# A two-layer decoder trunk: the opening norm taken channel by channel on transposed x, and the first residual read back from a stored copy

## The chip, the core and the metric

The kernel runs on one core of a Trainium2 chip. The metric is the device time of one execution in microseconds (us), and a kernel's time is the median of its runs. Engines are named as the profile names them: TensorE (PE; its weight loads are PEld), VectorE (DVE), ScalarE (ACT), GpSimd (POOL) and SyncE (SP), which only issues transfers.

## The reference, cut to what matters

`x` is 1024 positions by 1024 channels in float32. The trunk has two layers: a mixer and a gated MLP each, every one with an RMS norm ahead of it and a residual add behind it. The change concerns the first norm, the first projection and the first residual.

```python
def rmsnorm(x, g):
    xf = x.astype(jnp.float32)
    y = xf * lax.rsqrt(jnp.mean(xf * xf, axis=-1, keepdims=True) + EPS)
    return (y * g.astype(jnp.float32)).astype(x.dtype)

def even_mixer(x, ...):                    # x is rmsnorm of the stream here
    p = x @ w_in                           # 1024 -> 2560
    xa, ga, c_pre, b_post, vb = jnp.split(p, ...)          # 512 channels each
    xa = causal_depthwise_conv(xa, lru_conv_w, lru_conv_b)
    ya = rg_lru(xa, ...) * jax.nn.gelu(ga)
    yb = b_post * causal_depthwise_conv(c_pre * vb, sconv_w, sconv_b)
    return jnp.concatenate([ya, yb], axis=-1) @ w_out

x = x + even_mixer(rmsnorm(x, mix0_norm), ...)
x = x + conv_glu_ffn(rmsnorm(x, ffn_norm[0]), ...)
# then the same with odd_mixer (gated chunks and attention), and a last norm
```

The norm's factor belongs to a position, its gain `g` to a channel.

## The kernel before, in words

**Layout.** Activations are kept channels by positions: 8 groups of 128 channels on the partitions, 1024 positions along the free axis, worked on in two halves of 512 (`HALF[0]`, `HALF[1]`). TensorE multiplies in a reduced format (`fp32r`), so every operand is split in two, a high part (a rounding copy on ScalarE) and a low part (the remainder, a subtraction on VectorE), and a product is three matmuls: high by high, high by low, low by high. The normed stream's parts are `AH` and `AL`, both 128x8x1024. A projection of 128 output channels over one half is `proj_half` (L376): 8 channel groups times 3 matmuls of 512 columns, 24 in all. Small accumulators come from four banks (`psml`), large ones from two pairs of banks (`pbig`). `t2` gives 4 buffers of 512 columns, `t4` gives 4 of 1024.

**Weights.** `W` walks a list of weights in the order of their use. Raw weights (`wst`, 512 KB, two buffers) are asked of SyncE's queue (L106), which takes its transfers in order; ScalarE makes `wh`, VectorE `wl` (L129), three pairs of buffers. `W.get(key, depth)` prepares that many weights ahead.

**What sets the order.** The text is run by a scheduler that orders each engine's queue by its own costs and by the tiles' dependencies; the order within an engine is then fixed. `tc.issue_after` pins an instruction behind another. In the start, the order is written by hand: the string `START` lists steps (`q` squares, `r` root, `s` scale, `h` high, `l` low, `w` a weight ahead) with a block of 128 positions, and `WARM` puts matmuls of the identity (`warm`, L470) behind some of them, beside 14 at the very beginning.

**The start (`class Start`).** `x` arrives as 8 blocks of 128 positions by 1024 channels. For each block: ScalarE squares it into `xn` with the row sum in `sss` (L433), the reciprocal root follows in five small steps (L438 to L442), and VectorE scales the block by the factor of each position and the broadcast row `g0` of gains (L446). TensorE transposes the normed block in eight 128x128 pieces into two banks `xp` (L455), ScalarE writes the high parts `AH` from there (L459), VectorE the low parts `AL` (L464). `mix0` multiplies the first two projections (`0xa` and `0ga`) in quarters of 256 positions for the first half, then blocks 4 to 7 are normed while the first half of a third projection, `0cp0a`, is multiplied; then the second half of `0xa` and `0ga`, and `0cp0b`.

**Behind the start.** For each of four channel blocks the mixer makes a convolution over positions (`xc`, L402 and three taps at L405), its parts `xh` and `xl`, two block-diagonal gates from them (`ra`, `ix`, L1347, by weights `gwa` and `gwx`), a GELU of `0ga` (`gg`, L1369), and the projections `0cp`, `0vb` and `0bp`. The gate weights are put together in `t2` buffers: GpSimd clears them and issues four small loads (L1332), then the split makes `gwha`, `gwhx` and the low parts.

**The first output projection (`out_proj0`).** Its input is `Y`, split again into `AH` and `AL` (L370); 8 blocks of 128 output channels for each half. `Out.residual(oc)` loads 128 channels of `x` for all positions into `xc` (L546), TensorE transposes them in eight pieces (`xr`, L550), and ScalarE copies them to the stream's tile `hT_o` (L551). The eviction adds the product to the residual in place and stores it to `hdr` in DRAM (L557, L558), a tile of channels by positions. The second layer's `Out(1)` loads its residual from `hdr` already.

Of the kernel before, what the change touches and what calls it, by code (L numbers as in the profile page):

```python
# [16 lines left out]
P = 128  # L17
# [4 lines left out]
NH = 8  # L22
HD = 64
# [32 lines left out]
START = "q0 r0 s0 q1 r1 s1 h0 q2 l0 r2 s2 h1 l1 w1 q3 r3 s3 h2 l2 w2 h3 l3".split()  # L56

WARM = {"h0": 3, "h1": 3}
# [25 lines left out]
class Weights:  # L84
# [12 lines left out]
    def _dma(self, n=None):  # L97
        n = n or NWST + (self.more is not None)
        while self.n_dma < min(self.n_conv + n, len(self.plan) if self.limit is None else self.limit):
            key, ap = self.plan[self.n_dma]  # L100
            k, m = ap.shape[1], ap.shape[2]
            if self.more is not None and self.n_dma % 3 == 2:
                w = self.more.tile([P, DC, P], F32, tag="wst2", name=f"wst{self.n_dma}")
            else:
                w = self.pool.tile([P, DC, P], F32, tag="wst", bufs=NWST, name=f"wst{self.n_dma}")
            self.nc.sync.dma_start(w[:, :k, :m], ap)  # L106
            self.raw.append((w, k, m))
            self.n_dma += 1
# [11 lines left out]
    def ahead(self, depth=3):  # L120
# [14 lines left out]
        return did  # L135

# [20 lines left out]
def trunk(ctx: ExitStack, tc: tile.TileContext, x, mix0_norm, mix0_w_in, lru_conv_w, lru_conv_b,  # L157
# [111 lines left out]
    def load_rows(name, groups):  # L269
# [8 lines left out]
        t = cp.tile([P, n], F32, name=f"par_{name}")  # L278
        return t, offs, raw, n

    def turn_rows(t, offs, raw, n):
        ps = psml("pt")
        pe.transpose(ps[:, :n], raw[:n, :], ident[:n, :n])
        dve.tensor_copy(t, ps[:, :n])
# [131 lines left out]
    g0 = spl.tile([P, D], F32, name="g0")  # L416
    xs_, last = [], {}

    class Start:


        def __init__(self):
            self.ss = spl.tile([P, DC, 4], F32, name="sss")
            self.ys, self.ps = {}, {}

        def load(self, tt):
            xt = spl.tile([P, D], F32, tag="x", bufs=5, name=f"x{tt}")
            nc.sync.dma_start(xt, x[tt * P:(tt + 1) * P, :])
            xs_.append(xt)

        def squares(self, tt):
            y = self.ys[tt] = t4(f"xn{tt}")
            return act.activation(y, xs_[tt], AF.Square, accum_out=self.ss[:, tt, 0:1]), None  # L433

        def root(self, tt):
            sm = self.ss[:, tt]
            v, r, q = sm[:, 1:2], sm[:, 2:3], sm[:, 3:4]
            dve.tensor_scalar(v, sm[:, 0:1], 1.0 / D, EPS, op0=ALU.mult, op1=ALU.add)  # L438
            a = act.activation(r, v, AF.Abs_reciprocal_sqrt)
            dve.tensor_tensor(q, v, r, op=ALU.mult)  # L440
            dve.scalar_tensor_tensor(q, q, -0.5, r, op0=ALU.mult, op1=ALU.mult)
            return a, dve.scalar_tensor_tensor(r, q, 1.5, r, op0=ALU.add, op1=ALU.mult)  # L442

        def scale(self, tt):
            y = self.ys[tt]
            return None, dve.scalar_tensor_tensor(y, xs_[tt], self.ss[:, tt, 2:3], g0,  # L446
                                                  op0=ALU.mult, op1=ALU.mult)

        def high(self, tt):
            y, self.ps[tt] = self.ys.pop(tt), []  # L450
            for q_ in range(2):
                ps = psml(f"xp{tt}{q_}")
                for i in range(4):
                    c = 4 * q_ + i
                    pe.transpose(ps[:, i * P:(i + 1) * P], y[:, c * P:(c + 1) * P], ident)  # L455
                src = ps.rearrange("p (i t) -> p i t", i=4)
                at = slice(0, P), slice(4 * q_, 4 * q_ + 4), slice(tt * P, (tt + 1) * P)
                self.ps[tt].append((src, at))
                last["act"] = act.copy(AH[at], src)  # L459
            return last["act"], None  # L460

        def low(self, tt):
            for src, at in self.ps.pop(tt):
                last["dve"] = dve.tensor_tensor(AL[at], src, AH[at].bitcast(F32), op=ALU.subtract)  # L464
            return None, last["dve"]

        def warm(self, n):
            ps = psml("warm")
            for _ in range(n):
                pe.matmul(ps[:, :P], ident, ident, start=True, stop=True)  # L470

        def first(self):

            self.warm(14)
            steps = {"q": self.squares, "r": self.root, "s": self.scale, "h": self.high,
                     "l": self.low, "w": W.ahead}
            before = [None, None]
            for step in START:
                with ExitStack() as after:
                    for ins in before:  # L480
                        if ins is not None:
                            after.enter_context(tc.issue_after(ins.ins))
                    did = steps[step[0]](int(step[1:] or 0))
                before = [new or old for new, old in zip(did, before)]
                if step in WARM:
                    self.warm(WARM[step])

        def second(self, beside):


            steps = {"q": self.squares, "r": self.root, "s": self.scale, "h": self.high,
                     "l": self.low}

            def do(ops, *behind):
                for op in ops.split():
                    with ExitStack() as after:
                        for ins in behind:
                            after.enter_context(tc.issue_after(ins.ins))
                        steps[op[0]](int(op[1]))

            behind = last["act"], last["dve"]
            do("q4 r4 q5 r5 s4 h4 l4 q6 r6 s5 h5 l5 q7 r7 s6 s7", *behind)
            do("h6 l6 h7 l7", beside(*behind))
            turn_rows(*par_rows)
            sp_cm.__exit__(None, None, None)

    norm = [Start()]
    for tt in range(4):
        if tt == 3:
            W._dma(1)  # L510
        norm[0].load(tt)
        if tt == 0:
            nc.sync.dma_start(g0, mix0_norm.partition_broadcast(P))
    W._dma()
    par_rows = load_rows("a", [
        (r1(mix0_norm), 8), (lru_conv_w[0].rearrange("k (c p) -> (k c) p", p=P), 16),
# [5 lines left out]
    (o_n0, o_lw, o_lb, o_ba, o_bx, o_lam, o_sw, o_sb, o_n1, o_fn, o_fin, o_gb) = o  # L522
    gcols = {"mix0": cols(par, o_n0), "mix1": cols(par, o_n1), "ffn0": cols(par, o_fn),
             "ffn1": cols(par, o_fn + 8), "fin": cols(par, o_fin)}
    for tt in range(4, 8):
        norm[0].load(tt)
    norm[0].first()


    class Out:  # L530


        def __init__(self, ly):
# [3 lines left out]
            if ly:  # L537
# [5 lines left out]

        def residual(self, oc):
            xc = t4(f"xc{oc}").rearrange("p (n c) -> p n c", n=DC)
            nc.sync.dma_start(xc, x[:, oc * P:(oc + 1) * P].rearrange("(n p) c -> p n c", p=P))  # L546
            for h in range(2):
                ps = psml(f"xr{oc}{h}")
                for i in range(4):
                    pe.transpose(ps[:, i * P:(i + 1) * P], xc[:, 4 * h + i], ident)  # L550
                act.copy(self.hT[:, oc, HALF[h]], ps)  # L551
# [16 lines left out]
    def out_proj0(y_rest):  # L568
# [3 lines left out]
        o_.residual(0)  # L572
        for oc in range(DC):
            w = W.get(f"0o0{oc}")
            if oc < DC - 1:
                o_.residual(oc + 1)
# [698 lines left out]
    def mix0(norms):  # L1275


        ws = [W.get(k, 1) for k in ("0xa0", "0ga0")]
        pxa, pga = pbig("0xa0"), pbig("0ga0")
        for s in (slice(0, H // 2), slice(H // 2, H)):  # L1280
            for p_, w in zip((pxa, pga), ws):
                proj_half(p_[:, s], w, s)
        pc = [psml("0cp0a")]

        def beside(a, d):
# [604 lines left out]
```

## Time and profile before

| | |
|---|---|
| median of 3 runs | 2132.75 us (2132.11, 2132.75, 2134.26) |
| the profiled execution | 2131.98 us, of which the trace's span is 2130.3 |
| granted TensorE clock, mean | 0.999 |
| TensorE busy | 2093.4 us, 98% of the span, 9673 instructions |
| VectorE busy | 1599.0 us, 75% |
| ScalarE busy | 1068.4 us, 50% |
| GpSimd busy | 75.4 us, 4% |
| moved by the transfers | 249.98 MB, a mean of 117 GB/s |

Of the span, 60 us are the start and the first channel block's first projections, 190 more the rest of the first mixer, and from 255 to some 350 runs the first output projection; the other five sixths are the two MLPs, the second mixer and the last norm, which the change's steps don't touch. A row of an instruction reads: start in us, duration, engine, line, operation, output<-inputs, shape, and in brackets how long the engine had waited and what ended the wait. A row of a group has a count, the minimum, median and maximum duration in ns, and the time from the first to the last. A row of a stretch has its bounds, its length, then busy time (and instructions) of PE, PEld, DVE, ACT and POOL, the granted clock, the share of the 16 DMA engines and the GB/s.

### The profile page before, as it was taken

The page shows a single profiled execution, that of the slowest core. Times are in us where ns is not written, and L with a number is a line of the kernel's source. Part 1 is how long each engine was busy: PE and PEld are TensorE (multiplying, and loading weights), DVE is VectorE, ACT ScalarE, POOL GpSimd, SP SyncE. Part 2 cuts the span into 40 slices and gives each one's busy share as a digit, 9 for nine tenths or more (in the row PEclk, how much of TensorE's full clock was granted, in tenths as well). Part 3 has the DMA queues.
Part 4 walks back from the last instruction along what each step waited for, and adds up shares of the span by engine and source line. Part 5 has one row for each costly group of instructions (what it writes and reads, how often), then busy time and mean ns, then how long its engine had stood idle before and what let it go on. Part 6 is the DMA issues. An engine that isn't in the chain of part 4 may idle for free. (4 is left out here: it accounts for less than half of the span.)

```text
span 2130.3 us, 25849 instructions
## 1 busy us (share of the span) xinstructions
PE 2093.4 (98%) x9673; PEld 1719.2 (81%) x9673; DVE 1599.0 (75%) x2290; ACT 1068.4 (50%) x1493; POOL 75.4 (4%) x121
## 2 busy tenths in 40 slices
PE   8999999999999999999999999999999999999998
PEld 7888888788888888888778888788788888878887
DVE  6655647998888777875566766868998888777875
ACT  5333534654555555333556575744655455555323
POOL 0000001000000000000111111101000000000000
PEclk9999999999999999999999999999999999999999
DMA  4111342333323267752221212442333233267732
GB/s 150 56 50 41 108 154 94 95 113 109 104 96 107 80 206 253 242 173 74 75 58 54 75 56 59 156 153 89 104 104 119 94 116 97 80 228 248 240 104 80
DMA packets 269318, 249.98 MB, mean 117 GB/s; under 512 B 10224, under 2 KB 222000, under 8 KB 269192
## 3 DMA queue, kind: packets, MB, share of 16 engines
q1 hardware_dynamic: 268856, 247.83, 36.5%
q8 instruction: 76, 1.25, 0.2%
q0 software_dynamic: 192, 0.30, 0.1%
q14 instruction: 50, 0.41, 0.1%
q10 hardware_dynamic: 144, 0.20, 0.0%
HBM read 181.93 MB, written 64.26 MB: 116 GB/s over the span
## 5 line engine op out<-in xcount | busy, mean ns | idle before, releaser
L129 ACT CAST wh<-wst 128x1024 fp32r<-128x1024 f32 (+1 forms) x87 | 86.3, 992 | 223.4 <-PE op L376 45.2
L129 DVE TENSOR_TENSOR wl<-wst,wh 128x1024 fp32r<-128x1024 f32 (+1 forms) x87 | 100.0, 1150 | 96.6 <-ACT wh L129 96.5
L676 PE MATMUL X<-TH,wh 128*128 128x512 f32 x384 | 150.0, 391 | 1.8 <-ACT u L1034 1.4
L676 PE MATMUL X<-TH,wl 128*128 128x512 f32 x384 | 149.7, 390 | 0.7 <-DVE wl L370 0.7
L676 PE MATMUL X<-TL,wh 128*128 128x512 f32 x384 | 149.4, 389 | 0.0
L369 ACT CAST wh<-wst 128x1024 fp32r<-128x1024 f32 x96 | 100.3, 1051 | 74.6 <-PE YZ L676 49.5
L370 DVE TENSOR_TENSOR wl<-wst,wh 128x1024 fp32r<-128x1024 f32 x96 | 116.5, 1218 | 11.9 <-ACT wh L369 11.9
L698 DVE SCALAR_TENSOR_TENSOR cg<-g,par_c,cg 128x1023 f32<-128x1023 f32 x88 | 112.8, 1281 | 7.3 <-ACT cg L692 6.1
L698 DVE SCALAR_TENSOR_TENSOR cv<-v,par_c,cv 128x1023 f32<-128x1023 f32 (+1 forms) x88 | 112.4, 1277 | 0.0
L676 PE MATMUL YZ<-AH,wh 128*128 128x512 f32 x240 | 93.5, 389 | 0.0
L676 PE MATMUL YZ<-AL,wh 128*128 128x512 f32 x240 | 93.4, 389 | 0.0
L676 PE MATMUL YZ<-AH,wl 128*128 128x512 f32 x240 | 93.4, 389 | 0.0
L1034 ACT COPY u<-X 128x512 f32<-128x512 f32 x40 | 23.6, 589 | 137.3 <-PE X L676 137.3
L676 PEld LDWEIGHTS X<-TH,wh 128*128 128x128 f32 x384 | 72.1, 188 | 18.6 <-ACT u L1034 2.6
L676 PEld LDWEIGHTS X<-TH,wl 128*128 128x128 f32 x384 | 72.1, 188 | 16.6 <-DVE wl L370 1.6
L676 PEld LDWEIGHTS X<-TL,wh 128*128 128x128 f32 x384 | 72.1, 188 | 14.8
L376 PE MATMUL op<-AH,wh 128*128 128x512 f32 x192 | 76.3, 398 | 0.6 <-ACT hT_o L551 0.6
L376 PE MATMUL op<-AH,wl 128*128 128x512 f32 x192 | 74.9, 390 | 0.0
L376 PE MATMUL op<-AL,wh 128*128 128x512 f32 x192 | 74.8, 389 | 0.0
L1056 DVE TENSOR_TENSOR v<-p,u 128x512 f32<-128x512 f32 x40 | 27.6, 691 | 57.6 <-ACT u L1049 57.6
L692 ACT ACTIVATE cg<-g,par_c 128x1024 f32<-128x1024 f32 x44 | 54.8, 1246 | 29.4 <-DVE g L1058 24.7
L1600 ACT ACTIVATE P<-P,sm 128x128 f32<-128x128 f32 (+3 forms) x64 | 49.7, 777 | 30.0 <-DVE sm L1597 29.6
(779 smaller groups left out, 6301.9 us busy)
## 6 DMA issues: line engine op xcount, KB each, us to landing
wst<-in_ffn_up_dram SPq DMA_DIRECT2D x88, 512.0 KB
br<-hids SPq DMA_DIRECT2D x56, 512.0 KB
wst<-in_mix_w_in_dram SPq DMA_DIRECT2D x40, 512.0 KB
wst<-in_mix_w_out_dram SPq DMA_DIRECT2D x32, 512.0 KB
hids<-cv SPq DMA_DIRECT2D x32, 512.0 KB
hdr<-hT_o SPq DMA_DIRECT2D x32, 256.0 KB
hids<-t SPq DMA_DIRECT2D x32, 256.0 KB
hd<-hdr SPq DMA_DIRECT2D x16, 512.0 KB
```

Of the source, the lines that this page charges most:

```text
L129: did = self.nc.scalar.copy(wh[:, :k, :m], w[:, :k, :m]), self.eng.tensor_tensor(wl[:, :k, :m], w[:, :k, :m], wh[:, :k, :m].bitcast(F32), ...
L369: return (act.copy(h, src), (eng or dve).tensor_tensor(l, src, h.bitcast(F32), op=ALU.subtract))
L370: (eng or dve).tensor_tensor(l, src, h.bitcast(F32), op=ALU.subtract))
L376: last_mm = pe.matmul(ps, a[:, k], b[:, k, s], start=(k == 0 and i == 0), stop=(k == DC - 1 and i == 2))
L676: last = pe.matmul(ps, a[:, k0 + k], b[:, k], start=(first and k == 0 and i == 0), stop=(k == 3 and i == 2), skip_group_check=True)
L692: act.activation(self.cg, self.g, AF.Identity, scale=taps[2](f), bias=bias(f))
L698: dve.scalar_tensor_tensor(dst[:, dl:], src[:, :T - dl], taps[j](c), dst[:, dl:], op0=ALU.mult, op1=ALU.add)
L1034: u2_ = act.copy(u2, X)
L1056: dve.tensor_tensor(v[:, HALF[1]], p5, u3, op=ALU.add)
L1600: act.activation(Pt[:, :n], Pt[:, :n], AF.Exp, bias=low, scale=-1.0, accum_out=sm[:, 6:7])
```

## The change

It has three parts.

**The start.** `x` is transposed as it is, block by block (L503), into `xT`, one tile of channels by positions for each half; VectorE copies the first half's pieces, ScalarE the second's. The squares' sums of a half's four blocks stay together (`ssm`), the root is taken once for the half (five small steps), and becomes a matrix: `diag` is four identities scaled by the four blocks' factors, and one matmul of all ones by `diag` spreads them, so that the bank `rb` holds each position's factor on every partition. From there the work goes by groups of 128 channels `c`: VectorE makes `y = xT * g[c] * rb` (L481), ScalarE `AH`, VectorE `AL`, and the products of `0xa` and `0ga` for this group follow at full width of 512, the third one (by the low part of the weight) deferred for groups to come by `LATE`. Squares and transposes of blocks 4 to 7 are placed between. Then the root and `rb` of the second half, `0cp0a`, and the second half's groups. There are 7 `warm` matmuls at the beginning instead of 14, 2 behind each block, and 5 and 7 around `rb`. All eight blocks of `x` have buffers of their own; the gains come as 8 rows of 128 that TensorE turns into columns (`gT`). The loads' order becomes `x0`, gains, `x1` to `x3`, two weights, `x4` to `x7`, parameter rows. The high parts of the three weights are written from `W.parts` at set places.

**The first residual.** `xT` is stored half by half to `hdr` (2 MB each), and `Out(0)` loads it from there in 16 transfers of 256 KB; `residual` with its loads, transposes and copies is gone. The loads are pinned behind the last weight transfer that had been asked for at that place in the text.

**Places of tiles.** The small tiles' lengths are rounded up (`LINE` is 32 floats), and `hT` of the upper half gets 8 floats more, so that the large tiles behind them all start at the same place modulo 128 bytes.

```diff
-START = "q0 r0 s0 q1 r1 s1 h0 q2 l0 r2 s2 h1 l1 w1 q3 r3 s3 h2 l2 w2 h3 l3".split()
-WARM = {"h0": 3, "h1": 3}
+SQUARES = {2: 5, 4: 6, 5: 7}
+LATE = {4: (0, 1), 5: (2, 3), 6: (4, 5), 7: (6, 7)}
...
-        t = cp.tile([P, n], F32, name=f"par_{name}")
+        t = cp.tile([P, -(-n // LINE) * LINE], F32, name=f"par_{name}")
...
-            tiles.insert(0, cm.__enter__().tile([P, 4, T], F32, name=f"hT{i}_{name}"))
+            t = cm.__enter__().tile([P, 4 * T + i * LINE // 4], F32, name=f"hT{i}_{name}")
+            tiles.insert(0, t[:, :4 * T].rearrange("p (c t) -> p c t", c=4))
...
+        def root(self, h, beside=()):
...
+            self.do("dve", lambda: dve.tensor_scalar(v, ss, 1.0 / D, EPS, op0=ALU.mult,
+                                                     op1=ALU.add))
+            self.act_(r, v, AF.Abs_reciprocal_sqrt)
...
+            d = self.diag = t2(f"diag{h}")
+            self.tt_(d.rearrange("p (n t) -> p n t", n=4),
+                     ident.unsqueeze(1).broadcast_to([P, 4, P]),
+                     r.unsqueeze(2).broadcast_to([P, 4, P]), op=ALU.mult)
...
+        def spread(self, h):
+            self.r = psml(f"rb{h}")
+            self.mm_(self.r, self.one, self.diag, start=True, stop=True)
+        def scaled(self, h, c):
+            y = self.y[c] = t2(f"y0{h}{c}")
+            self.stt_(y, self.xT[h][:, c], self.g[:, c:c + 1], self.r, op1=ALU.mult)
+            self.do("act", lambda: act.copy(AH[:, c, HALF[h]], y))
...
+        def run(self, pxa, pga, pcp):
+            lows = []
+            self.warm(7)
+            for tt in range(4):
+                self.squares(tt)
+                copies = self.turn(tt, False)
...
+            self.root(0, copies)
...
+            self.squares(4)
+            self.warm(5)
+            self.spread(0)
+            self.warm(7)
+            self.scaled(0, 0)
+            self.scaled(0, 1)
+            both = list(zip((pxa, pga), ws))
+            for c in range(DC):
+                self.low(0, c)
+                if c + 2 < DC:
+                    self.scaled(0, c + 2)
+                if c in (1, 3):
+                    self.do("dve", lows.pop(0))
+                for p_, w in both:
+                    self.products(p_[:, HALF[0]], w, 0, (c,), (0, 1))
...
+            self.do("dve", low)
+            self.store(0)
+            self.root(1)
+            self.spread(1)
+            self.products(pcp, wc, 0, range(DC), (0, 1, 2))
+            self.scaled(1, 0)
+            self.scaled(1, 1)
+            for c in range(DC):
+                self.low(1, c)
...
+                for p_, w in both:
+                    self.products(p_[:, HALF[1]], w, 1, (c,), (0, 1, 2))
+            self.store(1)
...
-            if ly:
+            with tc.issue_after(W.last.ins):
                 for s in HALF:
                     for c in range(DC):
                         nc.sync.dma_start(self.hT[:, c, s], hdr[:, c, s])
...
-        small = pl.tile([P, 40], F32, name="lsm")
+        small = pl.tile([P, 2 * LINE], F32, name="lsm")
```

The order of instructions on TensorE where the first half ends, before (the last products of `0ga`, the transposes of blocks 4 and 5, the first product of `0cp0a`):

```order
L376 MATMUL 0ga0_272<-AH_83,wl1_230 128x256
L455 MATMUL xp40_385<-ident_76,xn4_370 128x128 x4
L455 MATMUL xp41_391<-ident_76,xn4_370 128x128 x4
L455 MATMUL xp50_407<-ident_76,xn5_377 128x128 x4
L455 MATMUL xp51_413<-ident_76,xn5_377 128x128 x4
L376 MATMUL 0cp0a_369<-AH_83,wh2_430 128x512
```

and the same place of the changed kernel (the last products of the first half, the transposes of block 7, the spread of the second half's factors):

```order
L484 MATMUL 0xa0_153<-AH_83,wl0_243 128x512 x2
L484 MATMUL 0ga0_154<-AH_83,wl1_248 128x512 x2
L503 MATMUL xp70_397<-ident_76,x7_116 128x128 x4
L503 MATMUL xp71_402<-ident_76,x7_116 128x128 x4
L484 MATMUL rb1_420<-diag1_418,one_93 128x512
L484 MATMUL 0cp0a_155<-AH_83,wh2_362 128x512
```

The transposes have moved in among the products, and `rb1`, which needs the second half's root and diagonal, stands ahead of `0cp0a`.

ScalarE behind the second half's high parts, before (`wh3` is the weight of `0vb`, `wh4` and `wh5` the two after it, `lsm` small tables):

```order
L459 CAST AH_83<-xp71_480 128x4x128
L369 CAST gwha_587<-gwa_583 128x512
L369 CAST gwhx_595<-gwx_591 128x512
L1303 ACTIVATE lsm_547<-par_a_117 128x4
L1304 ACT_TABLE_LOAD
L1304 ACTIVATE lsm_547<-lsm_547 128x4
L129 CAST wh3_671<-wst3_233 128x1024
L402 ACTIVATE xc0_599<-0xa0_271,par_a_117 128x1024
L129 CAST wh4_677<-wst4_434 128x1024
L1369 ACT_TABLE_LOAD
L1369 ACTIVATE gg0_608<-0ga0_272 128x1024
L369 CAST xh0_604<-xc0_599 128x1024
```

and now:

```order
L544 CAST AH_83<-y017_503 128x512
L389 CAST gwha_578<-gwa_574 128x512
L389 CAST gwhx_586<-gwx_582 128x512
L130 CAST wh3_662<-wst3_287 128x1024
L1455 ACT_TABLE_LOAD
L1455 ACTIVATE gg0_599<-0ga0_154 128x1024
L1389 ACTIVATE lsm_538<-par_a_130 128x4
L422 ACTIVATE xc0_590<-0xa0_153,par_a_130 128x1024
L1390 ACTIVATE lsm_538<-lsm_538 128x4
L130 CAST wh4_668<-wst4_410 128x1024
L130 CAST wh5_674<-wst5_666 128x1024
L1463 COPY cpr0_601<-0cp0b_602 128x512
L389 CAST xh0_595<-xc0_590 128x1024
```

The GELU `gg0` now stands ahead of the convolution `xc0`, the casts of the gate weights still ahead of both; on TensorE the gates `ra`, which need `xh0`, have moved behind the first 26 products of `0vb`. The tiles `gwa` and `gwx` now get `t2` buffers that the second half's `y` have used before them, so GpSimd's clearing and loads come behind the low parts made from those.

SyncE's queue at the first output projection, before (`wst22` and `wst23` are the third and fourth of its weights):

```order
L106 DMA wst21_1579<-in_mix0_w_out_dram 128x8x128
L106 DMA wst22_1668<-in_mix0_w_out_dram 128x8x128
L546 DMA xc0_1814<-in_x_dram 128x8x128
L546 DMA xc1_1834<-in_x_dram 128x8x128
L106 DMA wst23_1728<-in_mix0_w_out_dram 128x8x128
L546 DMA xc2_1900<-in_x_dram 128x8x128
```

and now:

```order
L107 DMA wst22_1659<-in_mix0_w_out_dram 128x8x128
L107 DMA wst23_1719<-in_mix0_w_out_dram 128x8x128
L652 DMA hT1_o0_1792<-hdr_85 128x512 x7
L652 DMA hT0_o0_1796<-hdr_85 128x512 x8
L652 DMA hT1_o0_1792<-hdr_85 128x512
L107 DMA wst24_1825<-in_mix0_w_out_dram 128x8x128
```

The residual's 16 loads stand together behind the fourth weight of this projection and ahead of the fifth; the tile of the upper four channel groups (`hT1`) comes first, but for its last piece. Behind this projection the order is that of before on every engine.

More of the change, by code (lines that the diff above doesn't have):

```diff
@@ L469, in warm @@
             for _ in range(n):
[L470 to L503, printed above, removed]
+                self.mm_(ps[:, :P], ident, ident, start=True, stop=True)
@@ L521, in trunk @@
     par, o = par_rows[:2]
[L522 to L527, printed above, removed]
+    (o_lw, o_lb, o_ba, o_bx, o_lam, o_sw, o_sb, o_n1, o_fn, o_fin, o_gb) = o
+    gcols = {"mix1": cols(par, o_n1), "ffn0": cols(par, o_fn), "ffn1": cols(par, o_fn + 8),
+             "fin": cols(par, o_fin)}
     class Out:
```

178 lines of the change are left out of this document (116 added, 62 removed).

## The prediction

> **What bounds the kernel now.** I read the page first (share of each engine), then who waited for whom on TensorE in the first 300 us, then the timelines of the two places that the diff touches.
>
> ```profile
> PE 2093.4 (98%) x9673; PEld 1719.2 (81%) x9673; DVE 1599.0 (75%) x2290; ACT 1068.4 (50%) x1493; POOL 75.4 (4%) x121
> ...
> 60.00:80.00 20.00, 20.00 (x90) 16.51 (x89) 16.66 (x10) 10.04 (x12) 0.00 (x0) 1.00 0.10 27
> ...
> PE xp L455 <- DVE xn L446: 4.7, 3, 1.8
> PE 0cp0a L376 <- DVE AL L464: 2.3, 1, 2.3
> PE op L376 <- ACT hT_o L551: 0.6, 1, 0.6
> ```
>
> TensorE is busy 98% of the span, and in a stretch such as 60 to 80 us without a gap: there time goes only if matmuls go. The waits of TensorE (total, times, longest) lie in the start, up to 35 us, and one of 0.6 at the output projection. The order on every engine behind the first output projection is that of before, so two places count: the start up to the first `0vb`, and the output projection.
>
> ```profile
> 17.39 0.39 PE L376 MATMUL 0xa<-AH,wl 128*128 128x256 f32 x1 [1.00 <-DVE sss L438]
> ...
> 30.30 1.91 PE L455 MATMUL xp<-ident,xn 128*128 128x128 f32 x16
> 34.53 0.50 PE L376 MATMUL 0cp0a<-AH,wh 128*128 128x512 f32 x1 [2.33 <-DVE AL L464]
> ...
> 55.74 0.39 PE L376 MATMUL 0cp0b<-AH,wh 128*128 128x512 f32 x1
> 55.97 0.39 PE L376 MATMUL 0cp0b<-AL,wh 128*128 128x512 f32 x1
> ...
> 59.15 0.40 PE L1347 MATMUL ra<-xh,gwha 128*128 128x512 f32 x1
> ```
>
> Before, products run steadily from 17.39, with a 2.33 wait at `0cp0a`, and the three projections of channel block 0 end at 59.15. Starts of neighbouring full-width products lie 0.227 apart; that, not the 0.39 of a row, is what one costs.
>
> **The output projection: what goes.** Removed are 64 transposes `xr`, 16 copies and 8 loads.
>
> ```profile
> L550 PE MATMUL xr<-ident,xc x64: 270/272/328, 255.6 to 296.8; 128*128 128x128 f32 x64
> ...
> 254.74 1.21 DVE L1396 TENSOR_TENSOR Y<-xc,gg 128x1024 f32<-128x1024 f32 x1
> 255.63 1.91 PE L550 MATMUL xr<-ident,xc 128*128 128x128 f32 x16
> 255.87 4.29 DVE L370 TENSOR_TENSOR AL<-Y,AH 128x512 fp32r<-128x512 f32 x7
> ...
> 302.39 0.39 PE L376 MATMUL op<-AH,wh 128*128 128x512 f32 x1
> ```
>
> From the first `xr` to the first product of the eighth block are 302.39 - 255.63 = 46.8 us; seven blocks of 24 products at 0.227 are 38.1; the rest, 8.7, is transposes, the 0.6 wait and two small transposes of tap rows (0.3, which stay). So -8.4. They covered something: the seven subtractions `AL<-Y` begin only at 255.87 on VectorE, 0.6 each. Without the 16 transposes the first block wants the first `AL` at 255.9 and gets it at 256.5 (0.7), and later the cast of the last `Y` half costs some 0.25: +1.0. The planner puts eight products of the next block ahead of the last `AL`, which covers that one. Sum here -7.4; bounds -8.4 (no cover lost) and -6.4 (twice that lost).
>
> In place of the transposes 16 loads of 256 KB from `hdr` go into SyncE's queue behind the fourth output weight and ahead of the fifth. The upper tile's space is free at once, the lower's after `Y<-xc,gg` (256). VectorE's first eviction needed its residual at 267.8, and behind it waits the weight of block 3, wanted at 273; 4.2 MB at the 224 GB/s of the row below are 18.7 us from 248.9, that is 267.6, and the tiles of the first eviction are not the last. I cost the loads at nothing: the cover is TensorE's queue of converted weights, and it is gone when the loads end after 271.
>
> ```profile
> 260.00:280.00 20.00, 20.00 (x101) 16.66 (x100) 14.67 (x21) 9.49 (x16) 0.00 (x0) 1.00 0.76 224
> ```
>
> **The start: what replaces what.** Durations:
>
> ```profile
> 4.37 1.06 ACT L433 ACTIVATE xn<-x 128x1024 f32<-128x1024 f32 x1 [1.14 <-DMA x<-in_x_dram]
> ...
> 5.74 0.20 ACT L439 ACTIVATE sss<-sss 128x1 f32<-128x1 f32 x1 [0.22 <-DVE sss L438]
> ...
> 6.36 0.16 DVE L442 SCALAR_TENSOR_TENSOR sss<-sss 128x1 f32<-128x1 f32 x1
> ...
> 8.14 1.06 ACT L433 ACTIVATE xn<-x 128x1024 f32<-128x1024 f32 x1 [2.20 <-DMA x<-in_x_dram]
> 21.34 1.06 ACT L433 ACTIVATE xn<-x 128x1024 f32<-128x1024 f32 x1
> 22.66 1.06 ACT L433 ACTIVATE xn<-x 128x1024 f32<-128x1024 f32 x1 [0.17 <-DMA x<-in_x_dram]
> ...
> L459 ACT CAST AH<-xp x16: 567/592/630, 9.6 to 42.2; 128x512 fp32r<-128x512 f32 x16
> L464 DVE TENSOR_TENSOR AL<-xp,AH x16: 678/681/692, 11.5 to 43.2; 128x512 fp32r<-128x512 f32 x16
> 41.43 2.48 DVE L464 TENSOR_TENSOR AL<-xp,AH 128x512 fp32r<-128x512 f32 x4 [5.16 <-ACT AH L459]
> L355 DVE SCALAR_TENSOR_TENSOR hT_o<-hT_o,par_a,r_no x32: 737/743/1782, 318.5 to 1485.0; 128x512 f32<-128x512 f32 x32
> 20.66 1.21 DVE L129 TENSOR_TENSOR wl<-wst,wh 128x1024 fp32r<-128x1024 f32 x1
> ```
>
> First product. On ScalarE the square of `x4` stands ahead of all casts `AH`, so the first cast waits for the seventh 512 KB load. Loads of that size follow each other by 1.3 (21.34 to 22.66) to 1.9 (4.37 to 8.14 with one between); I take 1.55, nearer the pure stretch, since the gate weights no longer load here: `x4` at 4.37 + 6 x 1.55 = 13.7, square and its sum 1.25, cast 0.6, first product 15.6 (14.1 to 17.6). The root, the diagonal and the spread of the first half are ready by about 13, hidden behind that.
>
> Columns 0 to 3 are paced by VectorE: to the fifth `AL` it does five at 0.6, four scalings at 0.66 (0.74 less the 0.08 by which neighbours overlap), two weight remainders at 1.15, 8.0 in all, so column 4 starts at 23.6. TensorE has 5.4 us of work in that time (16 products, 16 transposes at 0.109: sixteen in 1.91 less the 0.27 of the last). Then 31 products and 16 transposes, 8.8: 32.4. Here the new `rb` spread stands ahead of `0cp0a` on TensorE and waits: copy of the last transposes 0.65, root 0.25, three small VectorE steps and a hop 0.85, diagonal 0.7, so it starts at 34.9 and ends at 35.35. Then 24 products of `0cp0a` (to 40.8), 48 of the second half (51.7; VectorE needs 1.26 a column, TensorE 1.36, so TensorE leads), `pt` 0.25, 24 of `0cp0b`: 57.4. That is 59.15 - 57.4 = -1.8 (bounds -3.3 and +0.3 by the first product).
>
> Gate weights. Their staging tiles now reuse buffers of the second half's `y`; memset, GpSimd's loads, casts, and behind them in ScalarE's queue the weight of `0vb`, the GELU `gg` that frees `0vb`'s bank, and the convolution that makes `xh`.
>
> ```profile
> 54.97 1.28 ACT L1369 ACT_TABLE_LOAD   x1
> 56.27 1.03 ACT L1369 ACTIVATE gg<-0ga 128x1024 f32<-128x1024 f32 x1
> 49.64 1.20 ACT L402 ACTIVATE xc<-0xa,par_a 128x1024 f32<-128x1024 f32 x1
> 57.19 1.04 ACT L369 CAST xh<-xc 128x1024 fp32r<-128x1024 f32 x1
> 51.26 1.27 DVE L405 SCALAR_TENSOR_TENSOR xc<-0xa,par_a,xc 128x1023 f32<-128x1023 f32 x1
> ...
> 2.36 1.51 POOL L1332 DMA_DIRECT2D gwa<-in_lru_wa_dram  x2
> ...
> DMA to landing us min/median/max: 6.8/7.0/7.2
> ...
> DMA to landing us min/median/max: 3.2/3.2/3.2
> ```
>
> The buffer of `gwa` is free at the sixth `AL` of the second half (44.1), so GpSimd issues the last load at about 47.4. Landing took 7.0 for these loads among the start's traffic and 3.2 for the load of `fraw` (the second landing row) in a quiet stretch; the stretch at 47 is quiet, so 3.2: 50.6, and the weight cast at 51.8, when its buffer is free anyway. Then table load, GELU (55.2), `xc` (56.6), three taps with two weight remainders between (each in the queue ahead of a tap): 63.4, `xh` 64.5, `xl` 66.0. TensorE arrives at `xh` after 26 products of `0vb`, at 57.4 + 5.9 = 63.3, and waits 1.2, then 0.4 for `xl`: +1.6. Bounds: 0, if the planner's two remainders slip behind a tap's wait; +5.1, with 7.2 for landing, when everything above moves by 3.5.
>
> The store of the first half's transposes (2 MB) goes ahead of the weight of `0cp0a` in SyncE's queue. That delays its cast by up to 2 us, in a time when ScalarE has the last transposes' copies still before it: nothing.
>
> The same place modulo 128 bytes: the tiles of the first mixer's inner pool move from 96 to 64. At nothing, since operands at 96 and at 64 cost the same now:
>
> ```profile
> 75.23 1.22 DVE L1393 TENSOR_TENSOR ig<-ig,r 128x1024 f32<-128x1024 f32 x1
> 82.67 1.21 DVE L129 TENSOR_TENSOR wl<-wst,wh 128x1024 fp32r<-128x1024 f32 x1
> ```
>
> **The sum.** -7.4 - 1.8 + 1.6 = -7.6. The profiled execution took 2131.98 (span 2130.3 and 1.7 around it), 0.8 under the median of three, so 2124.4 against that execution and 2125.2 against the median; I say 2124.6.
>
> **The clock.**
>
> ```profile
> 9.06:12.47 3.41, 1.59 (x15) 1.43 (x14) 2.77 (x7) 2.43 (x7) 0.00 (x0) 1.00 1.13 264
> 1364.15:1367.57 3.42, 3.38 (x12) 2.68 (x11) 3.30 (x13) 3.37 (x10) 0.42 (x1) 0.50 0.89 297
> ```
>
> The granted clock stayed at 1.00 in a stretch in which TensorE was busy 1.59 of 3.41 us, half of it transposes; it fell to 0.50 once, for 3.4 us. The Trainium skill's page "TensorE: Matmul & The Clock Gate" (Part 1, and Part 4 on the transpose) says that the full clock needs a window of some 3.4 us of activity and that transposes do not count for it as matmuls do. It speaks against this change, which halves the opening run of warm-up products and then offers mostly transposes up to the first product. The trace does not bear out its sharp form, but it shows no start with so few warm-up products. By the row the start is as above; by the rule it would be the third rival.
>
> **Rivals.** (1) Late gate weights: 7.2 for landing instead of 3.2. For it: it is what these very loads took; against it: they were 64 KB each among loads of 512. +3.5: 2128. (2) A faster start: loads every 1.3 us and no wait for `xh`: -1.5 - 1.6 against the sum, 2121.5. For it: `0ga`'s 21.34 to 22.66; against: the weights' rows are short runs. (3) Half clock up to the first products: the 14 passes of seven warm-ups at twice 0.1 us and three turns of 0.9 more push the first product by about 2: 2126.6. For it the rule, against it the row. (4) Slower than before: the `hdr` loads. VectorE's eviction stands ahead of the weight remainders, so each microsecond after 271 is one of TensorE's; it decides from a lower tile landing at 279, where the 7.6 are eaten; at 281, with `wst` behind them too, 2135. That needs under 140 GB/s for 4.2 MB, against the 224 of the row. (5) The products' saving does not come because the first mixer is VectorE-bound in its last block: the first output block waits for each `AL`, not just the first: 2129.5.
>
> **How the numbers follow.** Forecast 0.55; late gate weights 0.15; faster start 0.11; half clock 0.09; VectorE-bound 0.06; slower 0.04. A change under 0.2% (4.3 us, 2128.5 to 2137.0 around the median) can hardly be told from none. The forecast's own range is 2122.3 to 2127; with the rivals to 8 in 10, 2120.5 to 2128.8. Faster 0.86: all of the forecast, the faster start and the half clock, two thirds of the late weights and a sixth of the VectorE case; the same 0.11; slower 0.03, most of the fourth rival.
>
> **What would show it.** No `xr` rows, and blocks of the output projection 5.45 apart instead of 6.37; a first full-width `0xa` product near 15.6; a wait of about 2.5 of TensorE at `rb`, ended by VectorE's diagonal; `0cp0b` ending near 57.4; a wait of 1 to 2 at `ra` for `xh`, and GpSimd's gate loads near 46 us. I am wrong if the order of loads shifts the first product past 17.6, if `gg` comes after 57.4 so that `0vb` itself waits, or if an eviction of the first output block waits for a load.

## The result, and the profile after

The changed kernel is slower: 2155.81 us median of 4 runs (2154.01 to 2161.0) against 2132.43 of before, a ratio of 1.0112, 95% interval 1.0093 to 1.0131. The forecast was 2124.6. The profiled execution took 2161.0, the longest of the four, of which the span is 2159.3, 29.0 more than before. One execution of a later experiment, e_warm, took 3505.29 us at a mean granted clock of 0.556, and that kernel's median below leaves it out.

The shares on the page show no engine that has become the bound:

```profile
PE 2126.7 (98%) x9580; PEld 1719.4 (80%) x9580; DVE 1608.4 (74%) x2285; ACT 1062.2 (49%) x1478; POOL 74.9 (3%) x122
```

TensorE has 93 matmuls fewer and is busy 33 us longer. So the place to look is not its waits but what a matmul takes. The waits of TensorE up to 330 us confirm that (total, times, longest): together 7.0 us, where the same view of before has 10.7.

```profile
PE rb L484 <- DVE diag L478: 3.8, 2, 3.2
PE warm L484 <- POOL ident masks.py:199: 1.5, 1, 1.5
PE 0xa L484 <- DVE AL L478: 0.9, 3, 0.3
PE 0xa L484 <- ACT AH L544: 0.6, 1, 0.6
PE op L396 <- DVE AL L390: 0.2, 1, 0.2
```

In the stretch from 60 to 250 us TensorE does hardly anything but products, and it is busy all 190.00 us of it in both kernels. Before:

```profile
60.00:250.00 190.00, 190.00 (x839) 157.04 (x838) 104.95 (x72) 69.92 (x75) 0.00 (x0) 1.00 0.18 51
```

After:

```profile
60.00:250.00 190.00, 190.00 (x817) 153.12 (x816) 108.20 (x104) 68.11 (x71) 0.00 (x0) 1.00 0.17 50
```

At the same granted clock of 1.00, 817 matmuls took the time of 839: 2.7% more for each, in a part of the program whose products the change doesn't alter. The rows of the products of the two MLPs, by their tiles, say which ones. Before (count, minimum/median/maximum ns, first to last start):

```profile
L676 PE MATMUL X<-TL,wh x384: 387/389/397, 383.8 to 1883.6; 128*128 128x512 f32 x192
...
L676 PE MATMUL YZ<-AH,wl x240: 389/389/389, 398.2 to 1892.0; 128*128 128x512 f32 x120
```

After:

```profile
L776 PE MATMUL X<-TL,wh x384: 387/389/398, 386.4 to 1909.2; 128*128 128x512 f32 x192
...
L776 PE MATMUL YZ<-AH,wl x240: 390/393/405, 401.0 to 1917.7; 128*128 128x512 f32 x120
```

Same weights, same shape, same loop: products that stream `TL` cost what they did, products that stream `AH` are longer. Over the whole trace, the starts of some 5900 products of 512 columns that have `AH` or `AL` as an operand lie 232.8 ns from the next on average instead of 227.4 (distances over 260 ns, which hold a wait, left out), and those of products without either still some 227.

What sets `AH` and `AL` apart is their place. They lie in front of the small parameter tiles (`par`), the weights and the other large tiles behind. The rounding of lengths (`LINE`) made each of four tiles `par_c` 384 bytes long instead of 352. So everything behind moved by 128 bytes, and `AH` and `AL` did not. Modulo 128, `AH`, `AL`, the weights `wh` and `wl`, `TH` and `TL` start at 64 in both kernels. Modulo 256 they all start at 192 before; after, `AH` and `AL` start at 192 and the others at 64.

Next come the two places that the change means to alter. The last product ahead of the output projection, before:

```profile
255.39 0.39 PE L376 MATMUL 0bp<-AH,wl 128*128 128x512 f32 x1
```

The same and the first product of the eighth block, in the changed kernel:

```profile
263.44 0.39 PE L396 MATMUL 0bp<-AH,wl 128*128 128x512 f32 x1
...
303.43 0.39 PE L396 MATMUL op<-AH,wh 128*128 128x512 f32 x1
```

That is 40.0 us; before, the eighth block started at 302.39, 47.0 behind the last `0bp`. So 7.0 us are gained here, in spite of the slower products. And the start:

```profile
16.86 0.50 PE L484 MATMUL 0xa<-AH,wh 128*128 128x512 f32 x1 [0.62 <-ACT AH L544]
...
37.33 1.42 PE L484 MATMUL rb<-diag,one 128*128 128x512 f32 x2 [3.22 <-DVE diag L478]
37.87 1.31 PE L484 MATMUL 0cp0a<-AH,wh 128*128 128x512 f32 x1
...
62.10 0.39 PE L396 MATMUL 0cp0b<-AH,wl 128*128 128x512 f32 x1
```

`0cp0b` ends some 3.2 us later than before, not earlier. Two rows say why: ScalarE's cast of the weight of `0cp0`, and the granted clock behind the wait at `rb`.

```profile
31.74 1.05 ACT L144 CAST wh<-wst 128x1024 fp32r<-128x1024 f32 x1 [4.02 <-DMA wst<-in_mix_w_in_dram]
...
37.98:41.39 3.41, 3.41 (x9) 2.31 (x8) 2.58 (x4) 1.24 (x2) 0.00 (x0) 0.50 1.03 386
```

A second such stretch, 6.8 us at half clock from 795.7 where before had none, is part of why the profiled execution lies 5 us over the median:

```profile
795.74:802.56 6.82, 6.01 (x14) 4.77 (x15) 6.52 (x7) 4.67 (x9) 0.00 (x0) 0.50 0.76 244
```

### The profile page after: what moved, and what is told of

The parts are those of the page before. It is cut to its first block, busy times and chain, and to the rows that moved or that the text cites. A ratio compares the mean times of both kernels' runs of the same rounds, so it can differ in the third digit from the quotient of the medians.

```text
span 2159.3 us, 25660 instructions
## 1 busy us (share of the span) xinstructions
PE 2126.7 (98%) x9580; PEld 1719.4 (80%) x9580; DVE 1608.4 (74%) x2285; ACT 1062.2 (49%) x1478; POOL 74.9 (3%) x122
## 5 line engine op out<-in xcount | busy, mean ns | idle before, releaser
L390 DVE TENSOR_TENSOR wl<-wst,wh 128x1024 fp32r<-128x1024 f32 x96 | 116.7, 1220 | 16.9 <-ACT wh L389 16.8
L776 PEld LDWEIGHTS X<-TL,wh 128*128 128x128 f32 x384 | 72.1, 188 | 15.6
L776 PE MATMUL YZ<-AH,dl 128*128 128x512 f32 x160 | 63.2, 395 | 0.0
```

The lines of the kernel that those rows point to most:

```text
L390: (eng or dve).tensor_tensor(l, src, h.bitcast(F32), op=ALU.subtract))
L776: last = pe.matmul(ps, a[:, k0 + k], b[:, k], start=(first and k == 0 and i == 0), stop=(k == 3 and i == 2), skip_group_check=True)
```

## The experiments

Three theories stood. **1**: a product costs more when its two operands begin at different places modulo 256 bytes, and the rounding made them differ. **2**: the new start with its store, and the residual's loads, cost the time. **3**: the clock. Each run was timed beside runs of the kernel before on the same chip (medians 2133.3 to 2134.3 there); what is given is the ratio to those.

### The weights moved on by another 128 bytes

```diff
     AL = cp.tile([P, DC, T], F32R, name="AL")
+    cp.tile([P, 32], F32, name="pad")
```

In the changed kernel (a_pad128) all large tiles are at 192 modulo 256 again.

> The changed kernel with one unused tile of 128 bytes behind AH and AL, so that AH, AL, the weights and all other large tiles begin at 192 modulo 256 again, as before. Theory 1 (a product pays some 6 ns when its two operands begin 128 bytes apart modulo 256): products of AH and AL go back from 232-238 to 227 ns; about 5930 of them by 6.1 is 36 us off the profiled 2161, so 2121 to 2127. Rival 2 (the new start, its store and the residual's loads cost the time): nothing changes, 2150 to 2160. Rival 3 (the chip granted less clock): clock still below 0.998 and time above 2145.

Measured: 2128.46, ratio 0.9979 (0.9970 to 0.9987). 128 bytes that nothing reads or writes take 27 us off, and the kernel is now faster than before. The same stretch:

```profile
60.00:250.00 190.00, 190.00 (x838) 156.85 (x837) 112.78 (x107) 70.82 (x75) 0.00 (x0) 1.00 0.17 49
```

Theory 1 holds, theories 2 and 3 fall for the loss as a whole. The time lies 1.5 us above the expected range: by the starts, the products of `AH` and `AL` went from 232.8 back to 227.4 ns, which is 5.4 each where 6.1 was expected.

### The rounding alone, and the shift alone, in the kernel before

b_line is the kernel before with the third part of the change only:

```diff
-        t = cp.tile([P, n], F32, name=f"par_{name}")
+        t = cp.tile([P, -(-n // LINE) * LINE], F32, name=f"par_{name}")
...
-            tiles.insert(0, cm.__enter__().tile([P, 4, T], F32, name=f"hT{i}_{name}"))
+            t = cm.__enter__().tile([P, 4 * T + i * LINE // 4], F32, name=f"hT{i}_{name}")
...
```

> The kernel before with the change's third part alone: lengths of small tiles rounded up to 32 floats, 8 floats more for hT of the upper half. It moves the weights and everything behind them from 192 to 64 modulo 256 while AH and AL stay at 192. Theory 1: as b_pad128, 2158 to 2165. Rival (rounding up is harmless): 2132 to 2134.

Measured: 2161.57, ratio 1.0131 (1.0117 to 1.0144), some 28 us. The other kernels put an unused tile behind `AL` in the kernel before: 128 bytes (b_pad128), 256 (b_pad256), 64 (b_pad64), 192 (b_pad192).

> The kernel before with the unused tile of 128 bytes behind AH and AL, nothing else: AH and AL stay at 192 modulo 256, weights and the rest move to 64. Theory 1: its products of AH and AL slow from 227 to about 233; some 6100 of them, +33 to +38 us, 2165 to 2171. Rival 2 (start and residual): no change, 2132.

> The kernel before with 256 unused bytes behind AH and AL: weights move by 256, the same place modulo 256. Theory 1 with the modulus 256: no change, 2131 to 2134, products at 227. If the modulus is 512 or the plain distance counts: slower than 2140.

> The kernel before with 64 unused bytes behind AH and AL: the weights at 0 modulo 256, AH and AL at 192. Theory 1 if every difference costs as much as 128: 2158 to 2165; if the cost grows with the distance: 2140 to 2150; if only 128 costs (two halves of a 256-byte line): 2132 to 2135.

> The kernel before with 192 unused bytes behind AH and AL: the weights at 128 modulo 256, AH and AL at 192, so that the moving operand lies 64 behind the weights. By the single products (229.0 at 64, 227 at 0): some 6000 products of AH and AL by 2.1 is +12.6 us, 2143 to 2149, where 64 and 128 bytes gave 2162. Rival (any difference costs the whole kernel the same): 2158 to 2165.

| unused bytes | moving `AH` minus weights, modulo 256 | us | ratio (95% interval) |
|---|---|---|---|
| 64 | 192 | 2162.06 | 1.0130 (1.0114 to 1.0147) |
| 128 | 128 | 2161.79 | 1.0135 (1.0121 to 1.0149) |
| 192 | 64 | 2149.06 | 1.0067 (1.0050 to 1.0083) |
| 256 | 0 | 2133.23 | 1.0002 (0.9993 to 1.0011) |

The shift alone does all that the rounding does; 256 bytes cost nothing, 64 as much as 128, and 192 half of it. The expectation for 128 bytes was too high by some 5 us at its lower end (33 for 28). Most of these 5 lie in the second mixer: the 1056 full-width products of its projections lay 230.0 ns apart already before and lie 232.5 apart in b_pad128, so the shift costs them 2.5 and not 6. In the stretch from 60 to 250 us b_pad128 and then b_pad192 count

```profile
60.00:250.00 190.00, 190.00 (x820) 154.12 (x820) 101.16 (x68) 65.94 (x68) 0.00 (x0) 1.00 0.17 50
60.00:250.00 190.00, 190.00 (x832) 155.94 (x831) 103.90 (x71) 68.41 (x72) 0.00 (x0) 1.00 0.17 50
```

against 839 before: here a distance of 64 costs some third of what 128 costs, as the single products below had said. Over the whole kernel it is half, 2 us more than the 12.6 expected. The places of a product's own two operands don't give that: in b_pad192 the 2088 products that stream `TH` or `TL`, which lie behind the unused tile as the weights do, are 229.7 ns apart instead of 226.8, some 5 us in all. Why is open, as it is for the 230.0 of the second mixer; in the whole kernel the difference of places explains most of the cost, not all of it.

### Whose place counts: AH and AL moved instead

```diff
+    cp.tile([P, 32], F32, name="pad")
     AH = cp.tile([P, DC, T], F32R, name="AH")
```

a_front128 is the changed kernel with the tile in front: now `AH` and `AL` are at 64, the weights at 192.

> The changed kernel with the unused tile of 128 bytes ahead of AH and AL instead: AH and AL at 64 modulo 256, all weights and other large tiles at 192. Theory 1 (the difference of the two operands decides): still 128 apart, products of AH and AL at 232-238, time 2150 to 2161 like the changed kernel. Rival 1b (the weights' own place 64 is slow, 192 fast): as fast as a_pad128, 2121 to 2127.

Measured: 2158.57, ratio 1.0120 (1.0106 to 1.0134). Neither 64 nor 192 is bad by itself; it is the difference.

### Products by themselves

micro leaves the trunk out and does nothing but products of 512 columns in one execution, `M` streaming and `S` as weights, 96 for each pair of places: `case(m, s)` reads `M` m bytes and `S` s bytes behind a multiple of 256.

```diff
+    def case(m, s):
+        p = ps.tile([P, H], F32, tag="p", name=...)
+        for n in range(96):
+            a, b = 128 * (n % 8) + s // 4, 1024 * (n % 8) + m // 4
+            pe.matmul(p, S[:, a:a + P], M[:, b:b + H], start=n == 0, stop=n == 95)
```

> Products by themselves: x is copied to the output (the trunk is left out), then 96 products of 512 columns for each of 34 pairs of places, the moving operand M at m bytes and the stationary S at s bytes behind a multiple of 256, all else idle. Theory 1 (the difference modulo 256 counts): 227 ns wherever m = s modulo 256, 232 to 238 at a difference of 128, whichever of the two is moved, and something between at 32, 64 and 96. Rival 1b (each operand's own place counts): (64,64), (96,96) or (128,128) differ from (0,0), and (128,0) and (0,128) differ from each other. Rival 1c (it takes traffic of the other engines, not TensorE alone): 227 everywhere here.

In the names the letter behind `m` and the one behind `s` count the places 0, 32, 64, 96, 128, 160, 192, 224, 256 from `a` to `i`. The distance of two products is first to last start by 95.

```profile
L50 PE MATMUL mbsa<-M,S x96: 393/396/399, 61.8 to 84.0; 128*128 128x512 f32 x96
L50 PE MATMUL mcsa<-M,S x96: 388/392/398, 84.2 to 106.0; 128*128 128x512 f32 x96
L50 PE MATMUL mesa<-M,S x96: 392/394/398, 128.6 to 150.8; 128*128 128x512 f32 x96
L50 PE MATMUL misa<-M,S x96: 389/389/395, 218.3 to 239.8; 128*128 128x512 f32 x96
L50 PE MATMUL masc<-M,S x96: 393/396/399, 306.6 to 328.8; 128*128 128x512 f32 x96
L50 PE MATMUL mese<-M,S x96: 387/389/397, 571.9 to 593.4; 128*128 128x512 f32 x96
```

So (to 1 ns, as the starts are given in tenths) 234 ns with `M` 32 bytes ahead, 229 at 64, 234 at 128, 226 at 256, and 226 with both at 128; with `S` 64 ahead (192 modulo 256) 234. All 34 cases fall in line by the difference of `M` and `S` alone: 227 at 0, 229 at 64, 232 to 234 at the six others that were tried. Hardly another engine was at work meanwhile (none but 0.59 us of ScalarE from 100 to 110 us, and no transfers), so it takes no traffic but TensorE's own; rivals 1b and 1c fall. The guess of something between at 32 and 96 was wrong: these cost as much as 128.

### Which two reads

micro2, again without the trunk, asks whether a product's own operands count or the weights that are loaded for the next one.

```diff
+    case("own", [(0, 0), (128, 128)])      # in turn: own operands alike, next weights apart
+    case("next", [(0, 128), (128, 0)])     # own operands apart, next weights alike
+    case("wapart", [(128, 0)], 256)        # 256 columns
```

> Products by themselves again (x copied to the output, the trunk left out), 96 of each kind, to tell which pair of places counts. Case own: M and S of one product at the same place (both 0, then both 128, in turn), so that the weights loaded for the next product lie 128 from the columns that stream now. Case next: the other way round, one product's own operands 128 apart, the next weights at the place of the present columns. Theory 2 (the next weights are read while the present columns stream, and these two reads disturb each other): own slow at 232 to 234, next at 227. Rival (the two operands of one product count): own 227, next 232 to 234. Case halfm (M at 0 and 128 in turn, S at 0) and halfs (S in turn): 229.5 to 230.5 by both. At 256 columns: 120 when alike, 123 to 126 when 128 apart if each load costs once per product (6 ns), 123 if the cost goes with the columns.

```profile
L51 PE MATMUL base<-M,S x96: 388/389/390, 61.8 to 83.4; 128*128 128x512 f32 x96
L51 PE MATMUL apart<-M,S x96: 387/394/399, 83.6 to 105.8; 128*128 128x512 f32 x96
L51 PE MATMUL own<-M,S x96: 387/391/397, 106.0 to 127.7; 128*128 128x512 f32 x96
L51 PE MATMUL next<-M,S x96: 388/393/396, 127.9 to 149.8; 128*128 128x512 f32 x96
L51 PE MATMUL halfm<-M,S x96: 388/392/398, 150.0 to 171.8; 128*128 128x512 f32 x96
L51 PE MATMUL halfs<-M,S x96: 389/394/399, 172.1 to 194.1; 128*128 128x512 f32 x96
L51 PE MATMUL wbase<-M,S x96: 281/283/284, 194.4 to 205.8; 128*128 128x256 f32 x96
L51 PE MATMUL wapart<-M,S x96: 278/281/286, 205.9 to 217.1; 128*128 128x256 f32 x96
```

The first four are 227, 234, 228 and some 230 ns apart. Neither theory gives these; both pairs seem to count in part. `halfm` has 229 to 230 as expected, `halfs` 232, above the 230.5 that both theories allowed. At 256 columns there is no cost (120 and 118). What happens in the chip stays open; that the difference of places decides is shown, why is not.

### What the residual is worth

e_resid is a_pad128 with the transposes, copies and loads of the first residual put back and the loads from `hdr` taken out; the two stores of `xT` stay.

```diff
+        o_.residual(0)
         for oc in range(DC):
             w = W.get(f"0o0{oc}")
+            if oc < DC - 1:
+                o_.residual(oc + 1)
```

> a_pad128 with the first residual made as before: 64 transposes of x, 16 copies, 8 loads, no loads from the store. Theory (the removal is worth 7.0 to 7.4 us on TensorE): 2135 to 2136. Rival (removal hidden, or paid by the loads): 2128 to 2130.

Measured: 2138.63, ratio 1.0022 (1.0013 to 1.0031), by the ratios 9 us more than a_pad128 and some 2.6 over the expected range. From the last `0bp` to the first product of the MLP, in a_pad128:

```profile
257.74 0.39 PE L397 MATMUL 0bp<-AH,wl 128*128 128x512 f32 x1
...
370.43 0.39 PE L777 MATMUL X<-AH,wh 128*128 128x512 f32 x1
```

and in e_resid:

```profile
256.36 0.39 PE L397 MATMUL 0bp<-AH,wl 128*128 128x512 f32 x1
...
376.53 0.39 PE L789 MATMUL X<-AH,wh 128*128 128x512 f32 x1
```

112.7 against 120.2: 7.5 us at the place itself, as the theory had it. Before took as long there as e_resid, 120.0, as its row of the MLP shows:

```profile
375.42 0.39 PE L676 MATMUL X<-AH,wh 128*128 128x512 f32 x1
```

The other 1.5 to 2 of the medians lie behind it: from the first product of the first MLP to its first `dq000A`, the profiled e_resid takes 407.8 us and a_pad128 404.8. Why is open.

### The wait at rb, and the clock behind it

e_warm puts 24 warm-up matmuls in front of the second half's `rb` in a_pad128, e_order takes the wait away.

```diff
             self.root(1)
+            self.warm(24)
             self.spread(1)
```

> a_pad128 with 24 warm-up matmuls ahead of rb of the second half, in the 3.3 us in which TensorE waits there. Theory (the clock goes to half for 3.4 us behind that idle stretch): full clock at 37 to 41 us, 0cp0a takes 5.5 us instead of 6.9, 1.4 to 1.8 us less: 2126.5 to 2127. Rival (the stretch has nothing to do with TensorE's idleness): it stays, 2128.5.

Measured: 2129.5, ratio 0.9980 (0.9972 to 0.9989), no gain. The stretch behind the warm-ups ran at full clock, and yet:

```profile
33.76 5.62 PE L485 MATMUL warm<-ident 128*128 128x128 f32 x48 [0.21 <-ACT xT L470]
39.22 1.02 PE L485 MATMUL rb<-diag,one 128*128 128x512 f32 x2
...
33.80:37.20 3.40, 3.40 (x30) 3.40 (x31) 1.18 (x4) 1.48 (x4) 0.00 (x0) 1.00 0.74 239
37.20:40.60 3.40, 3.40 (x25) 2.84 (x24) 0.31 (x1) 0.00 (x0) 0.00 (x0) 1.00 1.03 385
```

The experiment was mis-sized: 24 calls are 48 passes and 5.4 us, more than the wait of 3.3. They ran past it and gave back what the clock brought (`rb` at 39.2 instead of 37.35). That the stretch at half clock follows TensorE's idleness fits, but one execution cannot show it: e_resid, with the same 3.3 us wait, had full clock from 37 to 41 us too. The Trainium skill's page "TensorE: Matmul & The Clock Gate" (Part 1) says that the gate looks at a free-running window of some 3.4 us and falls back to half after one without work. The length of the stretch, 3.41, agrees, and a window that doesn't start with the wait would explain why a wait of 3.3 is followed by it in some executions alone.

e_order moves three things in the start:

```diff
+                if c == 5:
+                    with tc.issue_after(W.last.ins):
+                        self.store(0)
+                if c == 7:
+                    self.root(1)
+                    self.spread(1)
                 if c % 2:
                     for copy in self.turn(4 + c // 2, True):
                         copy()
             self.do("dve", low)
-            self.store(0)
-            self.root(1)
-            self.spread(1)
```

> The changed kernel with 128 unused bytes (a_pad128: 2128.5) and three moves in the start: the store of the first half's transposes goes behind the weights of 0cp0 and 0vb in SyncE's queue, the second half's root ahead of the copies of block 7, its spread rb ahead of the transposes of block 7. Theory (the start loses 3.3 us to the wait at rb, whose root stands in ScalarE's queue behind a cast that waits for a weight behind a 2 MB store, and 1.4 us to a half-clock stretch that this wait brings): no wait at rb, no stretch at 37 us, 0cp0a from 34.4 instead of 38.4; 3.6 to 5.4 us less, 2123 to 2125, the gates perhaps waiting 1 to 2 us for xh instead. Rival (the store and the loads share the same bandwidth, so the order does not matter, or the wait moves to the second half's AL): 2127 or more.

Measured: 2124.13, ratio 0.9957 (0.9945 to 0.9969): 9 us faster than before, within the expected range and the fastest kernel of the study. As the three moves were made at once, the gain isn't divided among them. ScalarE's cast no longer waits, `0cp0a` starts 3.6 earlier than in a_pad128, at full clock, and the gates now wait 0.9 for `xh`.

```profile
27.81 1.05 ACT L144 CAST wh<-wst 128x1024 fp32r<-128x1024 f32 x1
...
34.84 0.48 PE L485 MATMUL 0cp0a<-AH,wh 128*128 128x512 f32 x1
...
PE ra L1437 <- ACT xh L390: 0.9, 1, 0.9
```

## Why the prediction was wrong, step by step

**The step that failed: "The same place modulo 128 bytes ... At nothing, since operands at 96 and at 64 cost the same now".** It priced the part by rows of VectorE, and looked for tiles whose place modulo 128 changes. The tiles that mattered don't change theirs. The rounding of `par_c` moved all weights by a whole 128 against `AH` and `AL`, and TensorE, whose 98% was the first line quoted, was not asked. The measured price is 28 us (b_line, b_pad128), and 27 from the other side (the changed kernel without the shift). None of the five rivals had it: the fourth, slower than before, expected that from the loads out of `hdr`; the range was built from the start and the output projection only. A bound was to be had: if an operand's place could cost 1% of a product, some 6000 products of 0.227 are 14 us either way.

**Output projection, -7.4: right.** Taking the transposes out gives 7.3 between a_pad128 and before by the rows above (112.7 against 375.42 - 255.39 = 120.0), and 7.5 against e_resid. The cover lost is the 0.7 for the first `AL`, as said. The loads from `hdr` cost nothing that TensorE shows; rivals 4 and 5 did not come.

**The start, -1.8 and +1.6, sum -0.2: measured +2.6** (the first `0bp` in a_pad128 starts at 75.73, before at 73.08).
- First product: 15.6 forecast, 16.9 in a_pad128 and 16.86 in the changed kernel, within its bounds. The loads of blocks and weights came slower than 1.55 apart: the square of `x4` starts at 15.22 in a_pad128, six loads behind the first at 4.40, which is 1.80 each.
- "That delays its cast by up to 2 us ... nothing": wrong. The 2 MB store ahead of the weight made ScalarE wait 4.0 at the cast, and behind it stood the square of block 7, four copies and the root. `rb` came at 37.35 instead of 34.9; 1.4 of that is the later first half, 1.0 the cast.
- The wait at `rb` is 3.2 to 3.3 for 2.5 forecast. The stretch at half clock behind it was foreseen in neither place nor size: 24 products of `0cp0a` took 6.9 us in a_pad128 instead of 5.45. The third rival had the clock at the first products, where it stayed at 1.00 (from 7.3 to 38.0 us in the changed kernel).
- The wait of 1.2 to 1.6 for `xh` did not come, with everything on TensorE later; in e_order, where it wasn't, 0.9 came. The first rival, late gate weights, did not come either: the loads of `gwa` landed in 2.4 to 2.5 us in the changed kernel, where the forecast had 3.2 and the rival 7.2.

**The sum without the places of tiles** is then some 7.4 gained and 2.6 lost, 4.8, for 7.6 forecast: the output projection came as forecast, and the start has the wrong sign; a_pad128 measured 2.8 to 6.4 (its interval).

## What to carry to other kernels

Two operands of a matmul are a pair: in a kernel that lives of 512-column products in this format, put the streaming tile and the weight tile at the same place modulo 256 bytes, and look at both again whenever a small tile between them changes its length. When TensorE is busy 98% and the time moves, count matmuls in a stretch without waits before and after; a changed cost of one shows there at once, and in no list of waits. A store that nobody waits for still stands ahead of a weight in its queue, and the engine that waits for the weight takes its whole queue along.

## What the runs showed of the hardware that was not expected

- The distance of `fp32r` products of 512 columns depends on the difference of the start bytes of the moving operand and the weights modulo 256: 227 ns at 0, 229 at 64, 232 to 234 at 32, 96, 128, 160, 192 and 224, with TensorE alone at work (micro); over the whole kernel a difference of 128 costs 1.3% (b_pad128). At 256 columns there is no such cost (120 ns alike, 118 apart, in micro2). By the Trainium skill's page "SBUF — State Buffer" (Operand start alignment) an operand has to start at a multiple of its element size; all these starts do, and the time depends on them all the same.
- The granted clock fell to 0.50 for 3.41 us at the end of a wait of TensorE of 3.2 to 3.4 us or just behind it in three profiled executions (the changed kernel, a_pad128, a_front128) and not in a fourth of nearly the same program (e_resid).
